# Each TensorE transpose as two 64-row halves in two row tiles and two PSUM banks, norm factors applied ahead of the transposes

## The chip, the cores and the metric

One Trainium2 chip, one of its cores. The metric is the device time of one execution in microseconds (us). The kernel before ran three times: 2349.4 us (median), 2349.32 and 2351.5 us. One more execution was profiled; its span is 2349.9 us.

## The reference, cut to what matters

A decoder trunk of two layers on 512 tokens of width 1024, in float32. Each layer is a half-step SwiGLU, then three kinds of attention side by side with gates, then a second half-step SwiGLU, each between two RMS norms:

```python
for l in range(DEPTH):                       # DEPTH = 2
    f = _swiglu(_rmsnorm(h, ffn1_pre_g[l]), ffn1_w_gate[l], ffn1_w_up[l], ffn1_w_down[l])
    h = h + 0.5 * _rmsnorm(f, ffn1_post_g[l])
    u = _rmsnorm(h, mix_pre_g[l])
    proj = u @ w_in[l]
    ...
    o_sb = _stick_breaking_attention(...)    # 8 heads of 64, causal
    o_fx = _forgetting_attention(...)        # 8 heads of 64, causal
    k_mem, v_mem = jnp.split(mem_n @ w_mem_kv[l], 2, axis=-1)
    o_mem = _memory_attention(...)           # 4 heads of 128, 256 memory rows
    ...
    h = h + _rmsnorm(merged @ w_out[l], mix_post_g[l])
    f = _swiglu(_rmsnorm(h, ffn2_pre_g[l]), ffn2_w_gate[l], ffn2_w_up[l], ffn2_w_down[l])
    h = h + 0.5 * _rmsnorm(f, ffn2_post_g[l])
```

`mem_n` is the RMS norm of the 256 memory rows with gain `mem_norm_g`.

## The kernel before, in words

Activations stand as 128 tokens x 1024 features (`hT`, four token tiles). A matrix product needs the features on the partitions, so each normed tile is turned on TensorE: `nc.tensor.transpose(out, in, ident)` loads a 128x128 block of the data as the stationary operand and streams the 128 columns of the identity matrix through it; the result lands in PSUM. This happens in these places:

- `Sub.turned` (L578 to L589): eight blocks for each token tile at each of six norms, tiles `uta`, `utb`, `utc`, `utx` (line L586); for the first two token tiles of the program the same is written out in `begin` (L1618).
- `mem_norm` (L1042): the 256 memory rows, 16 blocks a layer, tile `mt` (L1064).
- `transposed` (L1151): the attention weights of one causal head, ten blocks, tiles `pts` (stick-breaking) and `ptf` (forgetting), line L1158. There are 16 such heads of each kind in the program.
- `mem_head` (L1252): the weights of one memory head, eight blocks, tile `ptm` (L1285), eight heads in the program.
- two small ones, `vecs_t` (L126 and L127: 8 and 48 rows) and `pfl` (L1313: 8 columns).

Every operand of a matrix product is kept as two fp32r numbers, a high and a low part; `split` (L179) makes them: ScalarE (ACT) copies the source to the high part, which rounds it, and VectorE (DVE) subtracts that from the source. `mm3` (L204 to L208) then issues three matmuls, high x high, high x low, low x high. After a transpose the source of `split` is the PSUM bank. In `turned` a factor `RS = -16` is applied by `split` (`scale=RS`, L185 and L186), since `rstd` (L480) returns -2 times the reciprocal root of the sum of squares by one Newton step. In `mem_norm` the gain `memg`, by then on the partitions, is applied after the transposes by L1069 (ACT) and L1070 (DVE), 256 columns at a time.

PSUM is eight banks of 128 x 512 fp32: four with the tag `mm` for products that run long, four with the tag `z` for attention scores, transposes and some sums of the feed-forward. A bank is taken by `pbank("z", ...)`.

The order of the work on each engine comes from the queue `Q`: jobs made of matmul steps (weights of the next products) into which the chains of heads and norms are woven (`weave`, L438), each chain asking for a wait in microseconds of TensorE work (`W_SB1 = 5.5`, `W_FX1 = 4.7`) before its next part. A scheduler below that may still move an instruction by a few places. Transposes of one head are issued with `keep_in_program_order`. DMAs are issued in order by SyncE (SP).

Of the kernel before, what the change touches and what calls it, by code (L numbers as in the profile page):

```python
# [18 lines left out]
P = 128  # L19
EPS = 1e-6  # L20


@with_exitstack
def kernel(
# [68 lines left out]
    nc.vector.memset(eps_t[:], D * EPS)  # L93
    one_t = cst.tile([P, 1], F32, name="one_t")
# [17 lines left out]

    gain_srcs = (ffn1_pre_g, ffn1_post_g, mix_pre_g, mix_post_g, ffn2_pre_g, ffn2_post_g)

    memg = cst.tile([P, ND], F32, name="memg")
# [4 lines left out]
    def vectors():  # L120
        vecs, n = tmp("vecs"), L * 3 * ND
        nc.gpsimd.dma_start(vecs[0:ND, 0:P], mem_norm_g.rearrange("(d p) -> d p", p=P))
        nc.gpsimd.dma_start(vecs[0:n, P:2 * P], b_gate.rearrange("l (d p) -> (l d) p", p=P))
        yield 0.0
        pt = pbank("z", "vecs_t")
        nc.tensor.transpose(pt[:, 0:ND], vecs[0:ND, 0:P], ident[0:ND, 0:ND])  # L126
        nc.tensor.transpose(pt[:, P:P + n], vecs[0:n, P:2 * P], ident[0:n, 0:n])  # L127
        nc.scalar.copy(memg[:], pt[:, 0:ND])
# [351 lines left out]
    def rstd(st, a, b=None, beside=None):  # L480

        s, m, y, w = st[:, a:a + 1], st[:, 3:4], st[:, 4:5], st[:, 5:6]
        if b is None:
            nc.scalar.activation(y, s, AF.Ln, bias=eps_t[:])
            nc.vector.tensor_scalar(m, s, D * EPS, None, ALU.add)
        else:
            nc.vector.tensor_scalar(m, s, st[:, b:b + 1], D * EPS, ALU.add, ALU.add)
            nc.scalar.activation(y, m, AF.Ln)
            if beside is not None:
                beside()  # L490
        nc.scalar.activation(y, y, AF.Exp, scale=-0.5)

        nc.vector.scalar_tensor_tensor(w, m, y, y, ALU.mult, ALU.mult)
        nc.vector.scalar_tensor_tensor(y, w, -3.0, y, ALU.add, ALU.mult)
        return y

    class Sub:
# [80 lines left out]
        def turned(self, t):  # L578

            self.alloc()  # L580
            ts_ = slice(t * P, (t + 1) * P)
            for hf in range(2):
                pt = pbank("z", f"ut{self.name}_{t}_{hf}")
                for e in range(4):
                    d = 4 * hf + e
                    nc.tensor.transpose(pt[:, e * P:(e + 1) * P], self.fs[t][:, d * P:(d + 1) * P], ident[:])  # L586
# [24 lines left out]
    def ffn(l, src, wg, wu, wd, dst, name, spare, parked, plan, aside=None):  # L611
# [136 lines left out]
        def token_product(ci, up, n, uns):  # L748

            nm = f"{name}{'gu'[up]}_{ci}_{n}"  # L750
            if n in (0, 1, 2):
                st["c", ci, up, n] = [pbank("z" if n == 0 else "mm", f"pw{nm}_{e}") for e in range(2)]
# [109 lines left out]
        def product(at, uns):  # L862
# [7 lines left out]
            if first and n in (0, 2):  # L870
                st["b", SUM[n]] = [pbank("z", f"pd{name}_{n}_{e}") for e in range(2)]
# [14 lines left out]
            if n == 0:  # L886
                st["b", 1] = [pbank("z", f"pd{name}_1_{e}") for e in range(2)]
# [154 lines left out]
    def mem_norm(l, mn):  # L1042

        mn[:] = [stile([P, ND, M], "tri", f"mn{l}_{i}") for i in range(2)]
        raws = []
# [8 lines left out]
        for t in range(MT):  # L1054
            raw = stile([P, D], "v", f"mraw{l}_{t}", F32)
            nc.sync.dma_start(raw[:], mem[0, t * P:(t + 1) * P, :])
            nc.vector.tensor_scalar(raw[:], raw[:], mem_rstd[:, t, 1:2], None, ALU.mult)
            raws.append(raw)
        yield 0.0
        for i in range(ND // 2):  # L1060
            pt = pbank("z", f"mt{l}_{i}")
            for j in range(2):
                for t in range(MT):
                    nc.tensor.transpose(pt[:, j * M + t * P:j * M + (t + 1) * P],  # L1064
                                        raws[t][:, (2 * i + j) * P:(2 * i + j + 1) * P], ident[:])
            for j in range(2):
                d = 2 * i + j
                src = pt[:, j * M:(j + 1) * M]
                nc.scalar.activation(mn[0][:, d], src, AF.Copy, scale=memg[:, d:d + 1])  # L1069
                nc.vector.scalar_tensor_tensor(mn[1][:, d], src, memg[:, d:d + 1],  # L1070
                                               mn[0][:, d].bitcast(F32), ALU.mult, ALU.subtract)
            yield 0.45
# [78 lines left out]
    def transposed(ptile, name):  # L1151

        tri = tri_tile("pt" + name)
        for kt in reversed(range(NT)):
            pt = pbank("z", f"pt{name}_{kt}")
            for i in range(kt, NT):
                tc.keep_in_program_order(
                    nc.tensor.transpose(pt[:, i * P:(i + 1) * P], ptile[i][:, kt * P:(kt + 1) * P], ident[:]))  # L1158
            split(tri_part(tri, 0, kt), tri_part(tri, 1, kt), pt[:, kt * P:].rearrange("p (a b) -> p a b", b=P))
        return tri  # L1160
# [13 lines left out]
    def stick_head(q, k, vts, pj, j, cut, ot, name):  # L1174

        ptile = {}
        for rows in ((3,), (2,), (1, 0)):
            pz = pbank("z", f"z{name}_{rows[0]}")
# [42 lines left out]
    def fox_head(q, k, vts, pj, j, qk, ot, name, ahead):  # L1221
# [3 lines left out]
        pzs = [pbank("z", f"z{name}_{i}") for i in range(NT)]  # L1225
# [26 lines left out]
    def mem_head(q, ks, vs, hd, ot, name, begun):  # L1252
        scale = P ** -0.5
        pts = []
        for i2 in range(NT // 2):
            pz = pbank("z", f"z{name}_{i2}")
# [8 lines left out]
            nc.vector.tensor_reduce(st[:, 0:2], pz[:].rearrange("p (e m) -> p e m", e=2), AX.X, ALU.max, negate=True)  # L1265
# [13 lines left out]
        tri = stile([P, 2, MT * S], "tri", "pt" + name)  # L1279
        for kt in range(MT):  # L1280
            pt = pbank("z", f"pt{name}_{kt}")
            for i in range(NT):
                a = (i % 2) * M + kt * P
                tc.keep_in_program_order(
                    nc.tensor.transpose(pt[:, i * P:(i + 1) * P], pts[i // 2][:, a:a + P], ident[:]))  # L1285
            c = slice(kt * S, (kt + 1) * S)
            split(tri[:, 0, c], tri[:, 1, c], pt[:])
# [297 lines left out]
    def warm(n):  # L1585

        for _ in range(n):
            tc.keep_in_program_order(nc.tensor.matmul(wps[:], wsb[:, 0:P], wsb[:, 0:S], start=True, stop=True))

    def begin():  # L1590
# [21 lines left out]

        def turn(t, hf):
            ts_ = slice(t * P, (t + 1) * P)
            pt = pbank("z", f"utx_{t}_{hf}")
            for e in range(4):
                d = 4 * hf + e
                nc.tensor.transpose(pt[:, e * P:(e + 1) * P], sub.fs[t][:, d * P:(d + 1) * P], ident[:])  # L1618
            lows[t, hf] = split(sub.us[hf][:, :, 0, ts_], sub.us[hf][:, :, 1, ts_],
                                pt[:].rearrange("p (e q) -> p e q", e=4), scale=RS, later=True)  # L1620
# [60 lines left out]
    wps, wsb = pbank("z", "warm"), tmp("warm").bitcast(BF16)  # L1681
# [47 lines left out]
```

## Time and profile before

| what | value |
|---|---|
| median of 3 runs | 2349.4 us |
| the profiled execution: span, first to last instruction | 2349.9 us |
| TensorE matmul (PE) busy | 2337.9 us, 99% |
| weight loads (PEld) busy | 1977.6 us, 84% |
| VectorE (DVE) busy | 1799.9 us, 77% |
| ScalarE (ACT) busy | 1506.5 us, 64% |
| GpSimd (POOL) busy | 75.5 us, 3% |
| HBM | 143 GB/s over the span |

The profiled execution's span of 2349.9 us is 0.5 us above the median of the runs. A row of a group reads: line, engine, operation, `out<-in` by tile names (numbers left out), stationary rows x columns, shape of the moving operand, type and count. PE rows are the matmuls, PEld the weight loads that run ahead of them. A matmul's length on PE goes from its start to its modelled end and overlaps the next one; what an instruction of a stream costs is the distance from start to start. A timeline row gives start, length, and, for merged rows, the count behind an x.

### The profile page before, as it was taken

The page shows a single profiled execution, that of the slowest core. Times are in us where ns is not written, and L with a number is a line of the kernel's source. Part 1 is how long each engine was busy: PE and PEld are TensorE (multiplying, and loading weights), DVE is VectorE, ACT ScalarE, POOL GpSimd, SP SyncE. Part 2 cuts the span into 40 slices and gives each one's busy share as a digit, 9 for nine tenths or more (in the row PEclk, how much of TensorE's full clock was granted, in tenths as well). Part 3 has the DMA queues.
Part 4 walks back from the last instruction along what each step waited for, and adds up shares of the span by engine and source line. Part 5 has one row for each costly group of instructions (what it writes and reads, how often), then busy time and mean ns, then how long its engine had stood idle before and what let it go on. Part 6 is the DMA issues. An engine that isn't in the chain of part 4 may idle for free.

```text
span 2349.9 us, 30935 instructions
## 1 busy us (share of the span) xinstructions
PE 2337.9 (99%) x11623; PEld 1977.6 (84%) x11623; DVE 1799.9 (77%) x2359; ACT 1506.5 (64%) x2302; POOL 75.5 (3%) x134
## 2 busy tenths in 40 slices
PE   9999999999999999999999999999999999999998
PEld 7888888888888888888898888888888888888887
DVE  8877877577777688878798788766677766888785
ACT  6677465576766556775656775655777665567744
POOL 0000000000111000000000000000001100000000
PEclk9999999999999999999999999999999999999999
DMA  6667454223323554774646665532323235556744
GB/s 206 186 180 220 149 197 127 81 83 88 90 72 107 189 188 152 198 197 152 226 144 184 204 175 185 182 108 72 100 72 99 73 123 190 171 182 182 217 142 147
DMA packets 297849, 354.96 MB, mean 151 GB/s; under 512 B 78282, under 2 KB 189154, under 8 KB 297700
## 3 DMA queue, kind: packets, MB, share of 16 engines
q1 hardware_dynamic: 297604, 352.97, 49.0%
q8 instruction: 91, 1.49, 0.3%
q14 instruction: 58, 0.48, 0.1%
q0 software_dynamic: 96, 0.03, 0.0%
HBM read 319.39 MB, written 16.78 MB: 143 GB/s over the span
## 4 chain that ended last, share of the span: by engine, by line
PE 89%; DVE 3%; DMA 3%; ACT 3%; issue 2%; SPq 0%; DVEq 0%; ACTq 0%
PE pg L207 3%; PE pg L206 3%; PE pg L208 3%; PE pda L207 3%; PE pdc L207 3%; PE pda L206 3%; PE pda L208 3%; PE pdc L208 3%; PE pdc L206 3%; PE pq L207 1%; PE pq L206 1%; PE pk L207 1%; PE pb L208 1%; PE pk L208 1%; PE pq L208 1%
## 5 line engine op out<-in xcount | busy, mean ns | idle before, releaser
L206 PE MATMUL pg<-us_a,wh_wg 128*128 128x512 f32 x384 | 150.9, 393 | 0.0
L207 PE MATMUL pg<-us_a,wh_wg 128*128 128x512 f32 x384 | 149.7, 390 | 0.0
L208 PE MATMUL pg<-us_a,wl_wg 128*128 128x512 f32 x384 | 149.7, 390 | 0.0
L183 DVE TENSOR_TENSOR wl_da<-raw_da,wh_da 128x1024 fp32r<-128x1024 f32 x50 | 61.0, 1224 | 44.3 <-ACT wh_da L182 44.2
L183 DVE TENSOR_TENSOR wl_dc<-raw_dc,wh_dc 128x1024 fp32r<-128x1024 f32 x50 | 61.0, 1224 | 42.3 <-ACT wh_dc L182 42.3
L207 PE MATMUL pdc<-wl_dc,ahc 128*128 128x512 f32 x224 | 87.7, 391 | 0.0
L207 PE MATMUL pda<-wl_da,aha 128*128 128x512 f32 x224 | 87.6, 391 | 0.0
L208 PE MATMUL pdc<-wh_dc,alc 128*128 128x512 f32 x224 | 87.2, 389 | 0.0
L208 PE MATMUL pda<-wh_da,ala 128*128 128x512 f32 x224 | 87.2, 389 | 0.0
L206 PE MATMUL pdc<-wh_dc,ahc 128*128 128x512 f32 x224 | 86.5, 389 | 0.0
L206 PE MATMUL pda<-wh_da,aha 128*128 128x512 f32 x224 | 86.5, 389 | 0.0
L208 PEld LDWEIGHTS pg<-us_a,wl_wg 128*128 128x128 f32 x384 | 72.1, 188 | 15.1
L207 PEld LDWEIGHTS pg<-us_a,wh_wg 128*128 128x128 f32 x384 | 72.2, 188 | 14.1
L206 PEld LDWEIGHTS pg<-us_a,wh_wg 128*128 128x128 f32 x384 | 72.1, 188 | 14.1
L182 ACT CAST wh_da<-raw_da 128x1024 fp32r<-128x1024 f32 x50 | 52.3, 1051 | 45.6 <-PE pda L208 14.3
L182 ACT CAST wh_dc<-raw_dc 128x1024 fp32r<-128x1024 f32 x50 | 52.3, 1049 | 43.0 <-PE pdc L208 14.1
L186 DVE SCALAR_TENSOR_TENSOR wl_wg<-raw_wg,wh_wg 128x1024 fp32r<-128x1024 f32 x48 | 58.4, 1221 | 21.6 <-ACT wh_wg L185 21.6
L201 DVE SCALAR_TENSOR_TENSOR ga<-pg,bgate,ga 128x512 f32<-128x512 f32 x48 | 35.9, 748 | 48.4 <-ACT ga L200 48.4
L182 ACT CAST wh_uc<-raw_uc 128x1024 fp32r<-128x1024 f32 x44 | 46.3, 1053 | 38.4 <-PE pwc0g L208 9.1
L182 ACT CAST wh_ua<-raw_ua 128x1024 fp32r<-128x1024 f32 x44 | 46.2, 1053 | 31.7 <-PE pwa1g L208 8.6
L185 ACT ACTIVATE wh_wg<-raw_wg 128x1024 fp32r<-128x1024 f32 x48 | 50.6, 1057 | 24.5 <-PE pv L1119 11.7
L183 DVE TENSOR_TENSOR wl_uc<-raw_uc,wh_uc 128x1024 fp32r<-128x1024 f32 x44 | 53.8, 1222 | 16.2 <-ACT wh_uc L182 16.0
(643 smaller groups left out, 8015.9 us busy)
## 6 DMA issues: line engine op xcount, KB each, us to landing
raw_da<-in_ffn_w_down_dram SPq DMA_DIRECT2D x66, 512.0 KB, 4.8
raw_dc<-in_ffn_w_down_dram SPq DMA_DIRECT2D x66, 512.0 KB, 4.3
raw_ga<-in_ffn_w_gate_dram SPq DMA_DIRECT2D x52, 512.0 KB, 4.5
raw_ua<-in_ffn_w_up_dram SPq DMA_DIRECT2D x52, 512.0 KB, 4.5
raw_gc<-in_ffn_w_gate_dram SPq DMA_DIRECT2D x52, 512.0 KB, 4.2
raw_uc<-in_ffn_w_up_dram SPq DMA_DIRECT2D x52, 512.0 KB, 4.0
raw_wg<-in_w_gate_dram SPq DMA_DIRECT2D x48, 512.0 KB, 3.6
raw_wo<-in_w_out_dram SPq DMA_DIRECT2D x24, 512.0 KB, 3.4
```

Source lines behind the costliest of these rows:

```text
L182: both = [nc.scalar.copy(h_ap, src)]
L183: make = lambda: nc.vector.tensor_tensor(l_ap, src, h_ap.bitcast(F32), ALU.subtract)
L185: both = [nc.scalar.activation(h_ap, src, AF.Copy, scale=scale)]
L186: make = lambda: nc.vector.scalar_tensor_tensor(l_ap, src, scale, h_ap.bitcast(F32), ALU.mult, ALU.subtract)
L201: nc.vector.scalar_tensor_tensor(t, z, minus, t, ALU.max, ALU.add)
L206: nc.tensor.matmul(pt, lh, rh, start=start, stop=False, skip_group_check=free)
L207: nc.tensor.matmul(pt, lh, rl, start=False, stop=False, skip_group_check=free)
L208: nc.tensor.matmul(pt, ll, rh, start=False, stop=stop, skip_group_check=free)
```

## The change

1. `turn_tile` replaces the transposes: a 128x128 block is turned by two instructions, one for its upper 64 partitions, one for its lower 64. Each loads 64 rows x 128 columns and streams 64 columns of a 64x64 corner of the identity matrix. The two halves write the same columns of two neighbouring PSUM banks, 64 columns each.
2. So PSUM `z` is handed out in pairs of banks (`zpair`, two of them), and `zbanks` cuts single banks from pairs for the users that want those. `split` reads 64 columns from one bank and 64 from the other in turn (`turned_tiles`), and writes through `by_halves`.
3. `split` after a transpose has no factor any more: `rstd` gives the factor in full (`LIFT`), by the same number of instructions; the memory gain is fetched as a row for all partitions (`mg`, a DMA of SP in place of a small one of GpSimd) and multiplied in ahead of the transposes by L1087, a `scalar_tensor_tensor` in place of L1057's `tensor_scalar`.
4. A head's ten blocks go into two pairs, six blocks and four, and are split by three instructions on each of ACT and DVE where there were four.

```diff
+LIFT = 16.0 ** (1 / 3)
...
+    def zpair(name):
+        return ps.tile([P, 2, S], F32, tag="z", bufs=2, name=name)
+    def zbanks(n, name):
+        pairs = [zpair(f"{name}_{i}") for i in range((n + 1) // 2)]
+        return [pairs[i // 2][:, i % 2] for i in range(n)]
+    ROW_HALVES = (slice(0, P // 2), slice(P // 2, P))
+    def turn_tile(pair, n, src, hold=False):
+        for b, r in enumerate(ROW_HALVES):
+            ins = nc.tensor.transpose(pair[:, b, n * P // 2:(n + 1) * P // 2], src[r], ident[r, r])
+            if hold:
+                tc.keep_in_program_order(ins)
+    def turned_tiles(pair, n0, n1):
+        return pair[:, :, n0 * P // 2:n1 * P // 2].rearrange("p b (n q) -> p n b q", q=P // 2)
+    def by_halves(ap):
+        return ap.rearrange("p n (b q) -> p n b q", b=2)
...
-            nc.vector.tensor_scalar(m, s, D * EPS, None, ALU.add)
+            nc.vector.tensor_scalar(m, s, -1.0, -D * EPS, ALU.mult, ALU.add)
+            nc.scalar.activation(y, y, AF.Exp, scale=-0.5, bias=lift_t[:])
+            nc.vector.scalar_tensor_tensor(w, m, y, y, ALU.mult, ALU.mult)
+            nc.vector.scalar_tensor_tensor(y, w, 3.0 * LIFT * LIFT, y, ALU.add, ALU.mult)
+            return y
...
+            pair = zpair(f"ut{self.name}_{t}")
+            for d in range(ND):
+                turn_tile(pair, d, self.fs[t][:, d * P:(d + 1) * P])
             for hf in range(2):
-                pt = pbank("z", f"ut{self.name}_{t}_{hf}")
-                for e in range(4):
-                    d = 4 * hf + e
-                    nc.tensor.transpose(pt[:, e * P:(e + 1) * P], self.fs[t][:, d * P:(d + 1) * P], ident[:])
-                split(self.us[hf][:, :, 0, ts_], self.us[hf][:, :, 1, ts_],
-                      pt[:].rearrange("p (e q) -> p e q", e=4), scale=RS)
+                split(by_halves(self.us[hf][:, :, 0, ts_]), by_halves(self.us[hf][:, :, 1, ts_]),
+                      turned_tiles(pair, 4 * hf, 4 * hf + 4))
...
+        raws, grow = [], stile([P, D], "v", f"mg{l}", F32)
+        nc.sync.dma_start(grow[:], mem_norm_g.rearrange("(a d) -> a d", a=1).broadcast_to([P, D]))
...
-            nc.vector.tensor_scalar(raw[:], raw[:], mem_rstd[:, t, 1:2], None, ALU.mult)
+            nc.vector.scalar_tensor_tensor(raw[:], raw[:], mem_rstd[:, t, 1:2], grow[:], ALU.mult, ALU.mult)
...
-        for kt in reversed(range(NT)):
-            pt = pbank("z", f"pt{name}_{kt}")
-            for i in range(kt, NT):
-                tc.keep_in_program_order(
-                    nc.tensor.transpose(pt[:, i * P:(i + 1) * P], ptile[i][:, kt * P:(kt + 1) * P], ident[:]))
-            split(tri_part(tri, 0, kt), tri_part(tri, 1, kt), pt[:, kt * P:].rearrange("p (a b) -> p a b", b=P))
+        for at, kts in enumerate(((3, 2, 1), (0,))):
+            pair, n0, first = zpair(f"pt{name}_{at}"), 0, TRI[kts[-1]] // P
+            for kt in kts:
+                for i in range(kt, NT):
+                    turn_tile(pair, TRI[kt] // P - first + i - kt, ptile[i][:, kt * P:(kt + 1) * P], hold=True)
+            for a, b in ((3, 6), (0, 3)) if at == 0 else ((0, 4),):
+                h, low = (by_halves(tri[:, 1 + part * TRIW // P + first + a:1 + part * TRIW // P + first + b])
+                          for part in range(2))
+                split(h, low, turned_tiles(pair, a, b))
```

Where the order of instructions changes: the PE rows of the second stick-breaking head of layer 0 (`pts0_0_1`; `ts` are its weights, `pk` the product of a later pair of heads that runs around it). Before, its ten blocks follow one another:

```order
L208 MATMUL pk0_0_2_4282<-us_a0_0_2946,wl_k0_0_2_3945 128x512
L1158 MATMUL pts0_0_1_3_4291<-ident_65,ts0_0_1_3_4138 128x128
L1158 MATMUL pts0_0_1_2_4295<-ident_65,ts0_0_1_2_4149 128x128
L1158 MATMUL pts0_0_1_2_4295<-ident_65,ts0_0_1_3_4138 128x128
L1158 MATMUL pts0_0_1_1_4300<-ident_65,ts0_0_1_1_4162 128x128
L1158 MATMUL pts0_0_1_1_4300<-ident_65,ts0_0_1_2_4149 128x128
L1158 MATMUL pts0_0_1_1_4300<-ident_65,ts0_0_1_3_4138 128x128
L1158 MATMUL pts0_0_1_0_4306<-ident_65,ts0_0_1_1_4162 128x128 x2
L1158 MATMUL pts0_0_1_0_4306<-ident_65,ts0_0_1_2_4149 128x128
L1158 MATMUL pts0_0_1_0_4306<-ident_65,ts0_0_1_3_4138 128x128
L206 MATMUL pk0_0_2_4282<-us_a0_0_2946,wh_k0_0_2_3944 128x512
```

Now, the same place:

```order
L234 MATMUL pk0_0_2_4365<-us_a0_0_2973,wl_k0_0_2_4023 128x512
L131 MATMUL pts0_0_1_0_4374<-ident_65,ts0_0_1_3_4223 128x64 x2
L131 MATMUL pts0_0_1_0_4374<-ident_65,ts0_0_1_2_4233 128x64 x2
L131 MATMUL pts0_0_1_0_4374<-ident_65,ts0_0_1_3_4223 128x64 x2
L232 MATMUL pk0_0_2_4365<-us_a0_0_2973,wh_k0_0_2_4022 128x512
L131 MATMUL pts0_0_1_0_4374<-ident_65,ts0_0_1_1_4245 128x64 x2
L131 MATMUL pts0_0_1_0_4374<-ident_65,ts0_0_1_2_4233 128x64 x2
L131 MATMUL pts0_0_1_0_4374<-ident_65,ts0_0_1_3_4223 128x64 x2
L131 MATMUL pts0_0_1_1_4391<-ident_65,ts0_0_1_1_4245 128x64 x4
L131 MATMUL pts0_0_1_1_4391<-ident_65,ts0_0_1_2_4233 128x64 x2
L131 MATMUL pts0_0_1_1_4391<-ident_65,ts0_0_1_3_4223 128x64 x2
```

Twenty halves stand where ten blocks stood, and one matmul of another product now lies among them. In the whole program the 608 full blocks stood in 67 unbroken runs (10 blocks for a causal head, 8 for a memory head or a token tile, 4 + 12 and 16 for the memory rows); the 1216 halves stand in 74: four stick-breaking and two forgetting heads are cut in two as here, and the memory rows of each layer stand as 4 and 28 halves.

The second place is the start of SP's part for the memory rows of layer 0 (`raw_da`, `raw_mk`: weights; `mraw`: memory rows). Before:

```order
L250 DMA raw_da0_1_2_2549<-in_ffn1_w_down_dram 128x2x512
L1056 DMA mraw0_0_2724<-in_mem_dram 128x1024
L250 DMA raw_da0_1_4_2583<-in_ffn1_w_down_dram 128x2x512
L1056 DMA mraw0_1_2727<-in_mem_dram 128x1024
L250 DMA raw_mk0_0_0_2646<-in_w_mem_kv_dram 128x4x256
L250 DMA raw_mk0_0_4_2648<-in_w_mem_kv_dram 128x4x256
```

Now:

```order
L276 DMA raw_da0_1_2_2571<-in_ffn1_w_down_dram 128x2x512
L1075 DMA mg0_2737<-in_mem_norm_g_dram 128x1024
L276 DMA raw_da0_1_4_2605<-in_ffn1_w_down_dram 128x2x512
L1086 DMA mraw0_0_2745<-in_mem_dram 128x1024
L276 DMA raw_mk0_0_0_2665<-in_w_mem_kv_dram 128x4x256
L1086 DMA mraw0_1_2748<-in_mem_dram 128x1024
L276 DMA raw_mk0_0_4_2667<-in_w_mem_kv_dram 128x4x256
```

The gain row takes the first place of the memory rows, each memory row moves one place back, and the second of them now comes behind the first weights of the memory keys.

More of the change, by code (lines that the diff above doesn't have):

```diff
@@ L1224, in fox_head @@
         ptile = {}
-        pzs = [pbank("z", f"z{name}_{i}") for i in range(NT)]
+        pzs = zbanks(NT, "z" + name)[::-1]
         for i, pz in enumerate(pzs):
@@ L1254, in mem_head @@
         pts = []
-        for i2 in range(NT // 2):
-            pz = pbank("z", f"z{name}_{i2}")
+        pzs = zbanks(2, "z" + name)
+        for i2, pz in enumerate(pzs):
             for e in range(2):
```

68 lines of the change are left out of this document (32 added, 36 removed).

## The prediction

> **What bounds the kernel now.** First the span and clock of the core, then the busy times, then the engines' shares of the chain of work that ended last:
>
> ```profile
> core 0: 2349.9 us, clock 1.000
> ```
>
> ```profile
> PE 2337.9 (99%) x11623; PEld 1977.6 (84%) x11623; DVE 1799.9 (77%) x2359; ACT 1506.5 (64%) x2302; POOL 75.5 (3%) x134
> ```
>
> ```profile
> PE 89%; DVE 3%; DMA 3%; ACT 3%; issue 2%; SPq 0%; DVEq 0%; ACTq 0%
> ```
>
> TensorE is busy for all but 12 us of 2349.9, at full clock, and nine tenths of the last chain run on it. So what counts is how long each piece of its stream takes from start to start; a saving on VectorE or ScalarE is worth nothing unless TensorE waits for it. Next, everything that uses the identity matrix (min/median/max in ns, first and last start):
>
> ```profile
> L1158 PE MATMUL pts<-ident,ts x160: 270/272/327, 458.7 to 1793.8; 128*128 128x128 f32 x160
> L1158 PE MATMUL ptf<-ident,pf x160: 270/272/273, 645.1 to 1930.0; 128*128 128x128 f32 x160
> L586 PE MATMUL uta<-ident,fa x64: 270/273/273, 345.9 to 1529.9; 128*128 128x128 f32 x64
> L1285 PE MATMUL ptm<-ident,pm x64: 270/272/273, 393.8 to 1590.2; 128*128 128x128 f32 x64
> L1227 PE MATMUL zf<-causal,ident x64: 219/219/229, 636.0 to 1920.1; 128*128 128x128 bf16 x64
> L586 PE MATMUL utb<-ident,fb x64: 270/272/273, 833.2 to 2024.3; 128*128 128x128 f32 x64
> L1064 PE MATMUL mt<-ident,mraw x32: 270/273/330, 326.7 to 1492.6; 128*128 128x128 f32 x32
> L586 PE MATMUL utc<-ident,fc x32: 270/273/328, 1173.3 to 1191.6; 128*128 128x128 f32 x32
> L1618 PE MATMUL utx<-ident,fx x16: 421/421/476, 8.5 to 13.1; 128*128 128x128 f32 x16
> L586 PE MATMUL utx<-ident,fx x16: 270/272/273, 20.1 to 27.0; 128*128 128x128 f32 x16
> ...
> its engine sat idle before it (us, times) until:
>   DVE mraw L1057: 0.5, 1
> ```
>
> Without the bf16 row (no transpose) these are 160+160+64+64+64+32+32+16+16 = 608 full blocks, and in all of them TensorE waited 0.5 us. One run of ten in the timeline, between two products:
>
> ```profile
> 644.85 0.39 PE L208 MATMUL pb<-o,wl_wb 128*128 128x512 f32 x1
> 645.09 1.25 PE L1158 MATMUL ptf<-ident,pf 128*128 128x128 f32 x10
> 646.09 0.36 PE L1117 MATMUL pv<-wh_v,us_a 128*128 128x256 f32 x1
> 646.29 0.28 PE L1118 MATMUL pv<-wl_v,us_a 128*128 128x256 f32 x1
> ```
>
> Ten blocks take 1.25 us to the end of the last, which is 0.27 long: (1.25 - 0.27) / 9 = 0.109 us from start to start. The second pv matmul starts 1.20 after the first block; ten times 0.109 leave 0.11 for the pv matmul ahead of it, about its own step. So a run costs ten steps and nothing at its ends: loads run ahead beneath the matmuls. The transposes hold 608 x 0.109 = 66.3 us, 2.8% of the time: the most the change can touch.
>
> **What a half will cost.** What sets 0.109, the load of the block or the stream of the identity? The small transpose pfl answers: its stationary operand has 8 columns, its stream the same 128.
>
> ```profile
> 579.61 0.60 PE L1313 MATMUL pfl<-ident,fl 128*8 128x128 f32 x4
> ```
>
> (0.60 - 0.27) / 3 = 0.11 us: almost nothing to load, and the same step. So the stream sets it, and 64 columns should take 0.054. The load and the ends of a run come from the one place of this trace where a transpose has fewer than 128 rows, the vecs transposes of 8 and of 48 rows:
>
> ```profile
> 312.09 0.39 PE L208 MATMUL pda<-wh_da,ala 128*128 128x512 f32 x1
> 312.40 0.13 PEld L126 LDWEIGHTS vecs_t<-ident,vecs 8*128 8x128 f32 x1 [0.35 <-issue]
> 312.40 0.22 PE L126 MATMUL vecs_t<-ident,vecs 8*128 8x8 f32 x1
> 312.56 0.13 PEld L127 LDWEIGHTS vecs_t<-ident,vecs 48*128 48x128 f32 x1
> 312.56 0.26 PE L127 MATMUL vecs_t<-ident,vecs 48*128 48x48 f32 x1
> 312.75 0.19 PEld L206 LDWEIGHTS pda<-wh_da,hida 128*128 128x128 f32 x1
> 312.75 0.50 PE L206 MATMUL pda<-wh_da,hida 128*128 128x512 f32 x1
> 312.85 0.19 PEld L207 LDWEIGHTS pda<-wl_da,hida 128*128 128x128 f32 x1
> ...
> 313.08 0.39 PE L207 MATMUL pda<-wl_da,hida 128*128 128x512 f32 x1
> ```
>
> Here loads no longer run ahead. A product step is 313.08 - 312.85 = 0.23, so the stream ahead ends at 312.32; the first small load starts at 312.40, 0.08 to 0.09 later. Product L206 is loaded from 312.75 and gets going at 312.85, where the next load begins: 0.105 of load in the open. A block's load has a row of 0.13 where that one has 0.19, so it takes 0.055 less the rounding. Check: 8 rows take 0.055 + 0.007 of stream + 0.09 = 0.15 (seen 0.16), 48 rows 0.055 + 0.04 + 0.09 = 0.185 (seen 0.19). So each change between the full array and fewer rows empties the array, 0.09 us. A run of halves then costs, beyond its steps, 0.09 + 0.055 on entering, 0.09 + 0.105 on leaving: 0.34 us. There are 74 runs: **+25.2 us**, a cost the 67 runs of now do not have. Below this lies zero, if the 0.09 belongs to something peculiar to vecs (rival three); above, 0.39 a run, with the longer load.
>
> The step of a pair of halves has no row. Its floor is 0.055, if both halves load and stream side by side; twice that, 0.11, if the second half's load starts only when the first half's matmul does, which is how load and matmul alternate in every row above; 0.22 if nothing overlaps. I take 0.058, near the floor, since the halves share neither rows nor bank: 608 x 0.058 = **35.3 us** in place of 66.3.
>
> That choice is where a rule decides and no run here shows it: the Trainium skill, TensorE: Matmul & The Clock Gate, Part 3, has loads for other rows pulled ahead and the tiles' matmuls start about 4 ns apart, which gives 0.055 + 0.004 = 0.059 and a sum within 1 us of mine; without it the sum is rival one's.
>
> **The rest of the change.** The splits read two banks in turn, and a head's first one waits for six blocks instead of one. The cover is in the same head:
>
> ```profile
> 647.42 1.38 ACT L182 CAST ptf<-ptf 128x128 fp32r<-128x128 f32 x4
> ...
> 648.73 1.67 DVE L183 TENSOR_TENSOR ptf<-ptf,ptf 128x128 fp32r<-128x128 f32 x4
> ...
> 651.57 1.46 PE L1144 MATMUL pvf<-ptf,v 128*128 128x256 f32 x8
> ```
>
> ScalarE comes to the first split 1.3 us after the run has ended, other work being ahead of it; VectorE is done at 650.40 and TensorE reads at 651.57, 1.2 us later. Cost nothing; with that cover gone at most six pairs, 0.35 us, a head: 11 us for 32 heads. One split fewer per head on either engine, and `rstd` with as many instructions as before: nothing, since TensorE does not wait there. Pairs of banks hold as many banks as before: nothing. One vecs transpose goes: -0.2 us.
>
> The memory rows cost something. The gain multiplies them on VectorE in a three-operand form:
>
> ```profile
> 325.45 1.42 DVE L1057 TENSOR_SCALAR mraw<-mraw,mem_rstd 128x1024 f32<-128x1024 f32 x2
> ```
>
> ```profile
> L569 DVE SCALAR_TENSOR_TENSOR hfa<-fa,nfa,hfa 128x1024 f32<-128x1024 f32 x8 | 10.3, 1284 | 0.1
> ```
>
> ```profile
> 319.43 3.06 SPq L250 DMA_DIRECT2D raw_mk<-in_w_mem_kv_dram  x2
> ```
>
> ```profile
> DMA to landing us min/median/max: 4.6/5.0/5.6
> ```
>
> Two at 1.28 in place of two in 1.42: the second row is ready 1.1 us later, and TensorE waited 0.5 us there before. Four product matmuls (0.9 us) now stand between the first two blocks and the rest. On SP the second row's DMA comes behind raw_mk, which went out at 319.43: out at 319.9, landed by 325, just ahead of VectorE's 325.45. Behind it in SP's queue only the next raw_mk and the saves of h move, by one issue of some 0.4 us; behind a late row VectorE would hold the evacuation of pda. GpSimd loses a small DMA: nothing. Between 0 and 2 us a layer, I take 0.5: **+1.0 us**.
>
> Sum, against the profiled span: 2349.9 - 66.3 + 25.2 + 35.3 - 0.2 + 1.0 = 2344.9; the median of the runs lies 0.5 below the span: **2344.4 us**, a gain of 0.2%, about what a measurement of this kernel can tell from no change. Its own range, with steps of 0.055 to 0.065 and the memory rows at 0 to 2 us: 2341 to 2350.
>
> **The rivals.** *One: the halves line up.* The change then does not do what it says. Each half waits for its own load, which starts with the matmul ahead: 2 x 0.055 = 0.11 a pair, 66.9 us, no gain, and the 25.2 us of the ends on top: +26.6 with the memory rows, 2376. It decides as soon as a pair costs over 0.066, where 608 pairs and the ends make up 66.3. For it: loads and matmuls alternate in every row here. Against: only that no row here has two row tiles in turn.
>
> *Two: a half's load is as long as a product's,* 0.105 in the open, though both halves load at once: 608 x 0.105 + 74 x 0.39 = 92.7, +27.2, 2377. By the Trainium skill, same page, LDWEIGHTS, a load takes its columns over 1.2 GHz, 107 ns for 128 columns whatever the rows; the rows of 0.13 against 0.19 speak against it for these loads.
>
> *Three: no emptying at the ends.* The 0.09 us belong to vecs (8 rows, a wait on a DMA), and loads run ahead as now: only the pairs are left, 2349.4 - 31.0 + 0.8 = 2319. Against: the same 0.09 three times, once on going back to the full array.
>
> *Four: coarser hand-over.* Pairs go as forecast, but splits and bank pairs come late by up to 0.35 us a head: 2345 to 2356. Against: the 1.2 us of cover.
>
> *Five: no overlap at all,* 0.22 a pair: 133.8 + 25.2 - 66.3 + 0.8, +93, 2443.
>
> **How the numbers follow.** Forecast 0.52, rival one 0.28, two 0.05, three 0.07, four 0.05, five 0.03. The forecast's own range crosses the 0.2% line (4.7 us): of its 0.52, 0.24 are faster, 0.26 the same, 0.02 slower. Faster: 0.24 + 0.07 = 0.31. Same: 0.26 + 0.01 of rival four = 0.27. Slower: 0.02 + 0.28 + 0.05 + 0.04 + 0.03 = 0.42. The range runs from 2341 to 2380: it must hold rival one, and leaves out three and five.
>
> **What would show it.** In the profile after: the start-to-start step of two halves in a run (0.058 here, 0.11 by rival one or two, told apart by the loads' rows: 0.13 or longer); a gap of 0.09 ahead of a run's first load and a product load in the open behind its last half; TensorE's idle time in total, unchanged but for some 0.1 us at mt; VectorE's splits still done before TensorE reads. The prediction is wrong if a pair's step is above 0.066, if the runs' ends cost under 0.2 or over 0.45 us, or if TensorE waits for splits.

## The result and the profile after

| | before | after |
|---|---|---|
| median of 4 runs | 2350.45 us (2349.32 to 2351.58) | 2410.07 us (2407.89 to 2414.05) |
| ratio to before, 95% interval | | 1.0252 (1.0239 to 1.0264) |
| span of the profiled execution | 2349.9 us | 2408.0 us |

The changed kernel is 59.6 us slower where a gain of 5 was forecast, and it lies outside the range. One execution of those behind the figures below, of the kernel with the scores ahead of the reads, took 6575.3 us, and its figures go by the other three. First the span and clock, the busy times, and the engines' shares of the chain that ended last, from the page of after:

```profile
core 0: 2408.0 us, clock 0.995
```

```profile
PE 2359.2 (98%) x12230; PEld 1958.3 (81%) x12230; DVE 1812.9 (75%) x2320; ACT 1507.9 (63%) x2261; POOL 78.6 (3%) x133
```

```profile
PE 73%; DVE 9%; ACT 8%; DMA 6%; issue 3%; SPq 0%; DVEq 0%; ACTq 0%
```

TensorE now lacks 48.8 us of its span where it lacked 12.0. VectorE and ScalarE, at 3% each of the chain before, hold 9% and 8%, and the clock has lost half a per cent: amid the run its record has six stretches of 3.41 us at half clock, which cost 10 us, and that of before has none. So TensorE waits, which the prediction had ruled out.

What was forecast of the halves themselves did come. The loads of all `ptf` halves in after (min/median/max in ns), then those of one run of ten blocks in the timeline:

```profile
L131 PEld LDWEIGHTS ptf<-ident,pf x320: 134/138/142, 666.2 to 1979.8; 64*128 64x128 f32 x160
```

```profile
665.69 0.19 PEld L234 LDWEIGHTS pb<-o,wl_wb 128*128 128x128 f32 x1
666.23 0.70 PEld L131 LDWEIGHTS ptf<-ident,pf 64*128 64x128 f32 x20 [0.35 <-PE pb L233]
667.00 0.19 PEld L1144 LDWEIGHTS pv<-wh_v,us_a 128*128 128x128 f32 x1
667.11 0.19 PEld L1145 LDWEIGHTS pv<-wl_v,us_a 128*128 128x128 f32 x1
```

Twenty loads take 0.70 us to the end of the last, which is 0.14 long. Ten pairs thus have nine steps in 0.56, 0.062 us each (forecast 0.058). The ends are there too. The product ahead streams until 665.69 + 0.22 + 0.23 = 666.14, as its load at 665.69 is followed by its matmul one step later; the first half is loaded 0.09 after that. The last pair's loads begin at 666.23 + 0.56 = 666.79, need 0.055, and stream for 0.055, to 666.90; the product's load follows 0.10 later, at 667.00, and lies bare for 0.11 before the next. In, out and the bare loads make up about the 0.34 forecast.

What was not forecast is in the list of waits (us in total, times, longest):

```profile
PE zs L1213 <- DVE ts L1227: 10.5, 16, 0.9
PE pda L232 <- ACT pda L918: 4.6, 2, 2.5
PE pdc L232 <- ACT pdc L918: 4.4, 2, 2.3
PE pts L131 <- ACT ts L1228: 4.3, 4, 2.0
PE pwa1g L232 <- DVE sa L814: 2.7, 1, 2.7
PE pwa0g L232 <- DVE sa L814: 2.2, 1, 2.2
PE pwc1g L232 <- DVE sc L814: 2.0, 1, 2.0
PE pwc0g L232 <- DVE sc L814: 1.7, 1, 1.7
```

These eight rows are 32.4 us. None of them was in the list of before, whose largest entries are 1.3 us, and none waits for a split after a transpose. Seven are users that cut single banks from a pair with `zbanks`: the attention scores `zs`, and the feed-forward's sums `pda`, `pdc` and `pw..g` (the letter names the norm, the digit the block of columns, g the gate). The eighth, `pts`, is transposes that wait for a head's last weights, which are made from the scores. A pair is one tile, so whoever writes one of its banks waits for the readers of both. At the scores, TensorE in before, then TensorE and VectorE in after:

```profile
435.60 1.45 PE L1183 MATMUL zs<-k,q 128*128 128x512 f32 x8
```

```profile
444.44 0.73 PE L1213 MATMUL zs<-k,q 128*128 128x512 f32 x3
...
451.74 0.39 PE L233 MATMUL pvm<-ptm,mv 128*128 128x512 f32 x1
452.63 0.62 PE L1213 MATMUL zs<-k,q 128*128 128x384 f32 x2 [0.50 <-DVE ts L1227]
```

```profile
451.88 0.69 DVE L1227 TENSOR_TENSOR ts<-zs,ts 128x512 f32<-128x512 f32 x1
```

The 384-wide scores of row tile 2 go to the second bank of the pair whose first bank holds row tile 3. They wait for the last read of that first bank, which ends at 452.57, 8 us after it was written. In before a head's eight score products stood together, each row tile's in a bank of its own. The true stop is longer than the row's 0.50: the product ahead streams until 451.74 + 0.23 = 451.97, so the next starts 0.66 later, since a wait counts only from a row's modelled end.

In the feed-forward, VectorE's adds and ScalarE's copies of a sum, first in before:

```profile
151.43 1.28 DVE L785 TENSOR_TENSOR sa<-sa,pwa0g 128x512 f32<-128x512 f32 x2
```

```profile
204.82 0.58 ACT L889 COPY pda<-pda 128x512 f32<-128x512 f32 x1
...
207.50 0.58 ACT L889 COPY pda<-pda 128x512 f32<-128x512 f32 x1
```

Then in after:

```profile
153.85 0.68 DVE L814 TENSOR_TENSOR sa<-sa,pwa0g 128x512 f32<-128x512 f32 x1
154.45 1.22 DVE L209 TENSOR_TENSOR wl_ga<-tga,wh_ga 128x1024 fp32r<-128x1024 f32 x1
155.58 0.68 DVE L814 TENSOR_TENSOR sa<-sa,pwa0g 128x512 f32<-128x512 f32 x1
```

```profile
213.05 0.58 ACT L918 COPY pda<-pda 128x512 f32<-128x512 f32 x1
213.57 1.04 ACT L208 CAST aha<-asa 128x1024 fp32r<-128x1024 f32 x1
214.51 0.58 ACT L918 COPY pda<-pda 128x512 f32<-128x512 f32 x1
```

In before the two adds went from 151.43 to 152.71 without anything between. Now another piece of work stands between the two reads, and TensorE, which needs only the first bank, waits for the second read. The copies stood apart in before too, but in time. TensorE has 24 products of `pga` ahead of its next `pda`, 5.6 us of work; in before the second copy ended 4.9 us behind the start of the first of them (208.08 - 203.15), in after 8.0 us behind it (215.09 - 207.07). What follows a wait is seen in the table of stretches (length, TensorE's busy time and instructions, then the others'; the third number from the end is the granted clock):

```profile
154.00:156.40 2.40, 0.19 (x1) 0.02 (x1) 2.40 (x4) 0.10 (x1) 0.00 (x0) 1.00 1.06 381
156.40:160.20 3.80, 3.79 (x10) 2.98 (x11) 2.49 (x3) 1.89 (x2) 0.00 (x0) 0.56 0.76 254
160.20:163.00 2.80, 2.80 (x14) 2.31 (x13) 2.77 (x3) 1.05 (x1) 0.00 (x0) 0.99 0.01 5
```

After a wait of 2.2 us the clock stands at about half for some 3.4 us, and TensorE issues 10 matmuls in 3.8 us where the next 2.8 hold 14. That costs half of 3.4, 1.7 us, nearly as much as the wait did.

### The profile page after: what moved, and what is told of

Read it like the earlier page. It is cut to its first block, busy times and chain, and to the rows that moved or that the text cites. A ratio compares the mean times of both kernels' runs of the same rounds, so it can differ in the third digit from the quotient of the medians.

```text
span 2408.0 us, 32018 instructions
## 1 busy us (share of the span) xinstructions
PE 2359.2 (98%) x12230; PEld 1958.3 (81%) x12230; DVE 1812.9 (75%) x2320; ACT 1507.9 (63%) x2261; POOL 78.6 (3%) x133
## 4 chain that ended last, share of the span: by engine, by line
PE 73%; DVE 9%; ACT 8%; DMA 6%; issue 3%; SPq 0%; DVEq 0%; ACTq 0%
PE pg L232 3%; PE pg L233 3%; PE pg L234 3%; PE pda L232 3%; PE pda L233 3%; PE pda L234 3%; PE pdc L232 2%; PE pdc L233 2%; PE pdc L234 2%; PE pb L232 1%; PE pb L234 1%; PE pb L233 1%; PE pq L232 1%; PE pk L232 1%; DMA raw_wo<-in_w_out_dram 1%
## 5 line engine op out<-in xcount | busy, mean ns | idle before, releaser
L209 DVE TENSOR_TENSOR wl_ua<-raw_ua,wh_ua 128x1024 fp32r<-128x1024 f32 x44 | 53.7, 1222 | 11.9 <-ACT wh_ua L208 11.9
```

The costliest lines, as they stand in the source:

```text
L209: make = lambda: nc.vector.tensor_tensor(l_ap, src, h_ap.bitcast(F32), ALU.subtract)
```

## The experiments

Theory W: the loss comes of two banks being one tile, so that TensorE waits for readers of the other bank. Rival R: it comes of the row tiles. Each ratio is to runs of the kernel before on the same chip. "The single-bank kernel" below is the second experiment's.

**Pairs with whole blocks.** The pairs stay, but each block is turned in one piece into the flattened pair:

```diff
-        for b, r in enumerate(ROW_HALVES):
-            ins = nc.tensor.transpose(pair[:, b, n * P // 2:(n + 1) * P // 2], src[r], ident[r, r])
+        ins = nc.tensor.transpose(flat[:, n * P:(n + 1) * P], src, ident[:])
```

> The changed kernel with one part undone: every transpose is a full 128x128 block again, but PSUM z is still handed out in pairs of banks, and the factors still come ahead of the transposes. Theory W (a pair is one tile for the program's waits, so an instruction on one bank of it waits for reads of the other; all the loss is there): the loss of 59.6 us stays, and the runs of halves, which gained about 5.7 us in the trace after, no longer do: 2416 us (2405 to 2425). Rival R (the two row tiles and their changes of mode cost the time): back to 2350 to 2355 us.

Measured 2409.08 us, ratio 1.0260 (1.0241 to 1.0279). Its waits:

```profile
PE zs L1214 <- DVE ts L1228: 10.2, 16, 0.8
PE pdc L233 <- ACT pdc L919: 5.4, 2, 3.0
PE pda L233 <- ACT pda L919: 4.5, 2, 2.3
```

Without a single half, the whole loss and the same waits are there. R falls. The 6 us that the halves were expected to be worth here did not show: this kernel is 1 us under the changed one, not 6 over it.

**Halves in single banks.** The halves stay, but a pair is two tiles of one bank each, split apart by one instruction a bank:

```diff
-        return ps.tile([P, 2, S], F32, tag="z", bufs=2, name=name)
+        return [pbank("z", f"{name}_{b}") for b in range(2)]
```

> The changed kernel with the other part undone: halves in two row tiles and two banks as changed, but the two banks are two tiles of one bank each, and all other users of z get single banks as before; a split reads one bank, 64 columns of every block. Theory W: no waits on a neighbour bank, so the forecast's own sum comes out, some 5 us below before: 2345 us (2340 to 2350). Rival R: 2400 us or more, as the changed kernel.

Measured 2347.43 us, ratio 0.9987 (0.9978 to 0.9996): 2.7 us under the 2350.13 of before on that chip, and faster than both kernels. TensorE's busy time in the first mixing layer, in after, then in the single-bank kernel:

```profile
400.00:800.00 400.00, 391.17 (x2282) 1.00 0.28 84
```

```profile
400.00:800.00 400.00, 400.00 (x2341) 1.00 0.33 99
```

The 8.8 us of idle time in after are none here. W stands: 2410.07 - 2347.43 = 62.6 us come of the pairs being one tile (by the two ratios to before, 62).

**Norm factors alone.** The kernel before with item 3 of the change and nothing else:

```diff
-            nc.vector.tensor_scalar(raw[:], raw[:], mem_rstd[:, t, 1:2], None, ALU.mult)
+            nc.vector.scalar_tensor_tensor(raw[:], raw[:], mem_rstd[:, t, 1:2], grow[:], ALU.mult, ALU.mult)
```

> The kernel before with one part of the change alone: the norm factors and the memory gain are applied ahead of the transposes; full blocks, single banks. Theory W: 0 to 3 us above before, from the memory rows: 2350 to 2354 us. Rival F (the factors or the memory gain's DMA on SP hold up the stream): above 2360 us.

Measured 2350.5 us, ratio 1.0002 (0.9993 to 1.0011). The factors cost nothing that can be measured.

**Scores ahead of the reads.** The changed kernel with a head's score products all issued before its first read (here the stick-breaking heads; the forgetting heads alike):

```diff
+        for rows, pz in zip(((3,), (2,), (1, 0)), pzs):
+            w0 = (rows[0] + 1) * P
             w = w0 + (len(rows) - 1) * P
```

> The changed kernel, with all score matmuls of a causal head issued ahead of the first read of its scores, so that no score matmul waits for reads of the neighbour bank; nothing else differs, and the sums of the feed-forward still wait on pairs. Theory W: the waits at zs (13 us), pts, ptf and pv (9 us) go, those at the feed-forward's sums (some 21 us, with the slowed clock some 30) stay: 2388 us (2380 to 2395). Rival R: no change, 2410 us.

Measured 2395.5 to 2401.3 us, ratio 1.0202 (1.0187 to 1.0218), so 12 to 14 us under the changed kernel where 22 were expected. Its waits:

```profile
PE pts L131 <- ACT ts L1230: 6.6, 8, 2.0
...
PE pv L232 <- DVE ga L227: 4.0, 2, 2.0
```

The `zs` row of 10.5 is gone, but `pts` grew from 4.3 to 6.6, with 2.5 more behind VectorE, and `pv` from 1.4 to 4.0: part of the wait moved to the next user of the pair. In sum these rows fell by only 3.1 us, from 16.2 to 13.1, so most of the 12 to 14 us cannot be read from them. The feed-forward's rows stayed.

**Halves for the causal heads alone.** Whole blocks everywhere but in the 32 runs of ten, single banks:

```diff
-            for i in range(kt, NT):
-                tc.keep_in_program_order(
-                    nc.tensor.transpose(pt[:, i * P:(i + 1) * P], ptile[i][:, kt * P:(kt + 1) * P], ident[:]))
+                for i in range(kt, NT):
+                    turn_tile(pair, TRI[kt] // P - first + i - kt, ptile[i][:, kt * P:(kt + 1) * P])
```

> Halves in single banks for the 32 runs of ten blocks of the causal heads alone; norms, memory rows and memory heads are turned as full blocks, each into one bank, as in the kernel before; factors ahead. Theory S (a block gains 0.109 - 0.0625 = 0.0465 us and each run's ends cost 0.34, so a run breaks even at 7.4 blocks): 32 x (0.465 - 0.344) = 3.9 us under the kernel before, 2346 (2344.5 to 2348); the kernel with halves everywhere and single banks, 2347.4, is 36 runs of mostly eight blocks away, which should change it by 1 us either way. Theory N (a run's ends cost nothing in the end, and what was seen at them is covered later): 320 x 0.0465 = 14.9 us under before, 2335. Theory H (halves cost more among heads than the ends show, by later splits): at or above 2350.

Measured 2348.3 us, ratio 0.9991 (0.9982 to 1.0000). Within 1 us of the kernel with halves everywhere, and far from the 2335 of free ends: a run of eight about breaks even, as far as two kernels measured on two chips can tell. Of the 3.9 us forecast for the tens 1.8 came; the interval, 0 to 4.2, holds both.

**One whole block more, amid a run or behind it.** In the single-bank kernel, in each of 32 runs, an extra 128x128 block that nobody reads (`kt == 2` puts it amid the run, `kt == 0` in its place behind the run):

```diff
+                if kt == 2:
+                    tc.keep_in_program_order(
+                        nc.tensor.transpose(pair[0][:, 3 * P:], ptile[NT - 1][:, kt * P:(kt + 1) * P], ident[:]))
```

> The kernel with halves in single banks (2347.4), and in each of the 32 runs of a causal head one full 128x128 block more, amid the run, behind its third block; it goes to unused columns of the first bank and nobody reads it. Theory S (each change between halves and full array empties the array): the block's own step of 0.109 and one more leaving and entering, 0.34 less what the smaller load saves, so 0.40 to 0.45 a run: 32 x 0.42 = +13.5 us, 2361 (2359 to 2363). Theory N (no cost at the ends): 32 x 0.11 = +3.5 us, 2351.

> The control to the one amid the run: the same extra full 128x128 block, unread, but behind the tenth block of each of the 32 runs, where the array is given back to 128 rows anyway. Theory S: only its own step, 32 x 0.11 = +3.5 us, 2351 (2349 to 2353), so 9 to 11 us under the kernel with the block amid the run. Theory N: the same time as with the block amid the run, within 1.5 us.

Measured 2357.59 us amid, ratio 1.0029 (1.0017 to 1.0042); 2348.76 behind, ratio 0.9992 (0.9983 to 1.0001). The same block costs 8.8 us more in the one place than in the other, 0.28 us a run. The loads of one run, with the block amid:

```profile
644.99 0.26 PEld L130 LDWEIGHTS ptf<-ident,pf 64*128 64x128 f32 x6 [0.35 <-issue]
645.32 0.14 PEld L1190 LDWEIGHTS ptf<-ident,pf 128*128 128x128 f32 x1
645.58 0.51 PEld L130 LDWEIGHTS ptf<-ident,pf 64*128 64x128 f32 x14
```

From the whole block's load to the next half's lie 0.26 us, more than twice its step of 0.109. The cost of changing between halves and the full array is so shown by itself, at slightly less than expected (8.8 us for 9 to 11).

**One row tile at a time.** The causal heads' upper halves first, then the lower ones, single banks:

```diff
-            for kt in kts:
+            for half in range(2):
+                for kt in kts:
```

> The kernel with halves in single banks (2347.4), but the blocks of the causal heads' runs (320 of 608) are turned upper halves first, then lower halves: six and six, then four and four, so that the same row tile is used again and again. If the step of 0.0625 us a pair comes of the two row tiles loading and streaming side by side, the steps here are those of one row tile: 0.055 to 0.065 a half if its next load still goes under its stream, so about 0.12 a pair and 2347.4 + 320 x 0.0575 = 2366 (2361 to 2370); 0.11 a half if it doesn't, 2347.4 + 320 x 0.16 = 2398. If side by side is not what gives it: 2347 within 2.

Measured 2352.73 us, ratio 1.0012 (1.0002 to 1.0022): 5.3 us over the single-bank kernel, not 19. The loads of one run in three stretches (the second column group counts loads):

```profile
644.58:644.76 0.18, 0.17 (x3) 1.00 0.82 285
644.76:645.20 0.44, 0.44 (x17) 1.00 0.24 82
645.20:645.40 0.20, 0.20 (x7) 1.00 0.00 0
```

A load counts in each stretch it reaches into. The first three go alone, one each 0.06 us, as fast as a pair goes otherwise. Then fourteen go in 0.44 us, two each 0.06 us, and the last three alone again. So the step does come of two row tiles side by side. What was missed is that TensorE does not keep to the order here. Six upper, six lower, four upper and four lower halves give three alone, seven pairs and three alone if each half starts together with one of the other row tile three places away. Only three at either end go alone, and the 5.3 us are 0.17 us a run.

**The feed-forward's reads.** In the single-bank kernel the two reads of a sum are swapped, then also tied: one column of the second bank is read again behind both, so that both banks come free together:

```diff
-            for e in range(2):
+            for e in reversed(range(2)):
...
+            elif SUM[n] == 0:
+                nc.vector.tensor_copy(tied[:, 1:2], pts[1][:, 0:1])
```

> The kernel with halves in single banks (2347.4); nothing is tied in pairs, but in the feed-forward the two banks of a sum are read (added, copied) in the order second, first, while TensorE goes on in the order first, second. So TensorE waits for the later of two reads at each such place, as it does when both banks are one tile. Theory W (the time lost in the feed-forward is that wait, and the clock windows behind waits of 2 us): most of the feed-forward's share of the loss comes back without any pair of banks: waits of 2 to 3 us at pwa0g, pwa1g, pwc0g, pwc1g, pda and pdc, some 15 to 20 us in all, and a half-clock window of 3.4 us behind several of them at 1.7 us each: 2372 (2362 to 2380). Rival V (that share comes from elsewhere: the order of the instructions, or the halves): within 4 us of 2347.

> The kernel with the feed-forward's reads swapped (2350.6), and behind each two reads of a sum one column of the second bank is read once more by the same engine into a column that nobody uses. So both reads wait for the products of both banks (the second bank's come last), and both banks come free together, behind the later read, as with a pair that is one tile; heads and transposes keep single banks. Theory P (what the feed-forward loses is the tie at its own sums, with all that follows in the other engines' order): waits of 2 to 3 us at pwa0g, pwa1g, pwc0g, pwc1g, pda, pdc come up, 2375 (2365 to 2380). Rival Q (the tie at these sums is covered, and the feed-forward's loss needs the rest as well: z handed out two pairs at a time over all users, and the other order of the instructions that this gives): within 4 us of 2350.6.

Measured 2350.62 us swapped, ratio 1.0002 (0.9993 to 1.0011), and 2351.81 tied, ratio 1.0006 (0.9996 to 1.0015). Rivals V and Q hold, and what theories W and P expected of these sums, 25 us, did not come: the later of two reads costs some 3 us, the tie 1 more, which is within the noise. ScalarE's copies of `pda` in the tied kernel:

```profile
209.88 1.06 ACT L927 COPY pda<-pda 128x512 f32<-128x512 f32 x2
```

Here both reads go together, and the second ends 6.4 us behind the first of the 24 `pga` products (210.94 - 204.53), against 8.0 in after. A tie that both reads leave soon costs little; what hurts in after is that the last read comes late.

**A pair in one read.** So, in the changed kernel, pairs and halves kept, the feed-forward reads a pair with one instruction:

```diff
-                for e in range(2):
-                    nc.scalar.copy(st["b", 1][e][:], pts[e][:])
+                nc.scalar.copy(st["two", 1][:], st["two", 0][:])
...
+            if SUM[n] == 0:
+                parts = [(st["both", ci, up][:].rearrange("p e (f q) -> p (e f) q", f=2), r, g)]
```

> The changed kernel (2410), pairs of banks and halves as they are, but where the feed-forward reads both banks of a pair (adds, copies and the activation of sum 0, the copies of pda and pdc) one instruction of 1024 columns reads the pair in place of two of 512, so that no other work can stand between the two reads on VectorE or ScalarE. Theory T (TensorE waits there because the second read stands behind another piece of work): the second read ends some 1 us earlier; waits at pwa0g, pwa1g, pwc0g, pwc1g (8.6 us for VectorE) and at pda and pdc (9.0) fall to about half, most of the half-clock windows behind them go (they follow waits of about 2 us and more): 9 us of waits and 5 to 10 of windows, 2393 (2388 to 2399). Rival L (the reads come late as a whole, split or not): within 4 us of 2410.

Measured 2384.08 us, ratio 1.0147 (1.0130 to 1.0164): 26 us back, more than theory T's 17. Its waits, and the copy:

```profile
PE zs L1219 <- DVE ts L1233: 10.5, 16, 0.9
PE pts L131 <- ACT ts L1234: 4.2, 3, 2.0
...
PE pdc L232 <- ACT pdc L924: 0.9, 1, 0.9
PE pda L232 <- ACT pda L924: 0.7, 2, 0.4
```

```profile
207.84 1.01 ACT L924 COPY pda<-pda 128x1024 f32<-128x1024 f32 x1
```

The four `pw..g` rows for VectorE are gone, `pda` and `pdc` fell from 9.0 to 1.6 us, and the heads' rows are as they were. The copy ends 5.8 us behind the first `pga` product (208.85 - 203.03), where after's second ended 8.0 behind it. It is not just undivided: it also starts 1.2 us earlier against that product than the first copy of after. (The other 4.0 us between 207.84 and 213.05 are delay that after's stream had gathered by then.) Why the program's order put after's copies so late is not settled.

**Waits on purpose.** The single-bank kernel, with the copies ahead of which TensorE waits made two to five times:

```diff
-                for e in range(2):
+                for e in [0, 1] * (2 + 2 * up + ci):
                     nc.scalar.copy(st["c", ci, up, 1][e][:], st["c", ci, up, 0][e][:])
```

> The kernel with halves in single banks (2347.4, no half-clock window amid the run), with waits put in on purpose: in the feed-forward the two copies of sum 0 to sum 1, for which TensorE waits next, are made two, three, four or five times over by ScalarE (two times for the first gate columns, five for the last up columns; the result is the same numbers), each further pair some 1.0 us. So TensorE waits at some 16 places, from about 1 to 4 us. Theory K (a wait of about 2 us and more lets the clock fall to half for a window of 3.4 us, whatever made the wait): the page's windows and the matmuls of 0.6 us show half-clock windows behind several of the waits over 2 us and behind none under 1.5 us; each costs 1.7 us on top of the wait, so time is 2347.4 + the waits + 1.7 x windows, 2375 to 2410. Rival C (the half-clock windows of the changed kernel belong to what else it does, halves or pairs): the waits appear and no window does; time is 2347.4 + the waits.

Measured 2423.67 us, ratio 1.0320 (1.0305 to 1.0336). Twelve waits came up, not 16: four of 2.6 us, four of 3.5, four of 5.9 to 6.5. One of its rows, and the clock around three waits, in stretches of 3.41 us laid where its record can change:

```profile
PE pwa0u L235 <- ACT pwa0u L787: 6.1, 2, 3.5
```

```profile
178.91:182.32 3.41, 0.91 (x5) 1.00 0.45 154
182.32:185.74 3.41, 2.40 (x6) 0.50 0.00 0
1028.83:1032.24 3.41, 1.75 (x8) 1.00 0.46 152
1032.24:1035.65 3.41, 1.57 (x7) 1.00 0.00 0
1035.65:1039.07 3.41, 3.41 (x17) 1.00 0.00 0
1288.24:1291.65 3.41, 1.61 (x8) 1.00 0.57 154
1291.65:1295.07 3.41, 2.62 (x11) 1.00 0.00 0
```

Behind ten of the twelve the matmuls run at half speed for a while, as behind the 3.5 us that end at 183.34. Behind two they do not: the 3.5 us that end at 1034.09 and the 2.6 us that end at 1292.44. Waits of 1.0 us (at `utb`) were followed by none. Theory K holds: the wait brings the half clock, whatever made it.

But its length alone does not decide. The clock in the record changes only on a grid of 3.41 us, which begins elsewhere in each execution, and what tells the cases apart is how long TensorE idles within one stretch of it. At 178.91 it idles for 2.50 of 3.41 us, and the next stretch is at half clock. The equally long wait to 1034.09 lies across a border, 1.67 us on one side and 1.85 on the other, and the clock stays; so does it for the 1.80 us at 1288.24. In all fourteen traces, without the first and last 20 us, 32 stretches at full clock were followed by half clock, and TensorE idled 1.89 us or more in each of them; in the stretches that full clock followed it never idled more than 1.85. In the first 20 us of four traces 1.1 to 1.4 us were enough, for a reason that stays open.

The waits are 49 us; the time is 76 over the single-bank kernel, so some 27 are left. The half clock lasted longer than expected, up to three stretches at one wait, and TensorE worked under it for 49 us in all, which costs 25; 0.16 us a wait under a modelled end makes up the other 2.

## Why the prediction was wrong

- **The step of a pair**, 0.058 forecast, is 0.062. The choice against rival one was right: one row tile alone steps at 0.06 a half, two together at 0.06 a pair. The Trainium skill, TensorE: Matmul & The Clock Gate, Part 3, which has the tiles start side by side, agrees with this trace. Its section on LDWEIGHTS, behind rival two, does not for these loads: 128 columns over 1.2 GHz are 107 ns, but here two loads and two streams share a step of 62 ns. (The product load that lies bare for 0.11 us does agree with it.)
- **The ends of a run**, 0.34 us forecast, were seen in the run shown and, by themselves, as 0.28 in the pair of kernels with an extra block. Rival three falls.
- **The memory rows**, +1.0 us forecast, cost nothing that can be measured.
- **The sum of these**, -5.0 us, was measured in single banks: -2.7 (interval -5.2 to -0.9). No run is cut there, so it has 68 runs of halves, not 74, and the forecast's own terms would give -7.1; with 0.062 us a pair and nothing for the memory rows, -5.7. So up to here the mechanism was right, but some 3 us of the gain are missing, and no run says where.
- **The step that failed** is "Pairs of banks hold as many banks as before: nothing". The number of banks was counted, and not what a bank waits for. A pair is one tile, and a write to one bank waits for the readers of both. That is +62.6 us. (A stick-breaking head, which takes three banks, now also holds two pairs, which are four; no run separates this from the waiting.) With it fell "TensorE does not wait there", on which the free splits and the free instructions of VectorE and ScalarE rested; it was true of the kernel before only.
- **Rival four** had the coarser hand-over, but looked only at the splits of a head, 0.35 us each, at most 11 us. The waits are at the scores and the feed-forward's sums, which the change touches by one word each (`zbanks`).
- **Where the 62.6 us lie.** 26.0 are the feed-forward's: they went when a pair was read in one instruction. The profiles account for 24.5 of them: its waits fell from 17.6 us to 1.6, and five of the six stretches at half clock, 1.7 us each, stood behind those waits. Of the other 36.6, the two mixing layers show 17.9 us of TensorE idle (8.8 in after's row of 400 to 800, 9.1 in the second layer). At some 23 stops another 0.16 us each lies under a modelled end (3.7), and one half-clock window adds 1.7. About 13 us have no row of their own and stay open; 4.5 of them come of comparing medians, as the two profiled executions, 2381.7 and 2349.6 us, differ by 32.1 only. That the scores' share can be undone by order was shown for 12 to 14 us only.

## What to carry to other kernels

When a change makes one tile of what were two, list everyone who takes from that pool and ask of each who else still reads the tile when it writes; the capacity being the same says nothing. If two banks must be one tile, read them with one instruction. And price a wait of TensorE that idles it for over 1.9 us of one 3.41 us stretch of the clock's record at its length and about 2 us more (1.7 each in after, 2.5 on average in the kernel with waits on purpose).

## What the runs showed of the hardware

- Half clock followed a 3.41 us stretch of the clock's grid in which TensorE idled 1.89 us or more, 32 times of 32, and never one with 1.85 us or less, without the first and last 20 us. So a wait of 2.2 us brought it (154.0 in after), and one of 3.5 us across a border did not (1034.09 in the kernel with waits on purpose). The Trainium skill, TensorE: Matmul & The Clock Gate, Part 1, has the clock fall after an idle window of about 3.4 us, and such windows run freely, without regard to the program. The windows of 3.4 us that begin elsewhere in each execution agree with it here; that a wait must fill one does not.
- Halves of two row tiles that stand three places apart in the order still ran side by side, and so ahead of their places.
- Changing between 64-row halves and the full array costs some 0.3 us each time in and out, so a run of transposes in halves gains only from about eight blocks on: eight about broke even, ten gained 0.06 us a run (0 to 0.13).
